# Splitting the first load of a streaming GLU kernel: 16 rows ahead of the launch barrier, 112 rows behind it

## The chip, the cores and the metric

The kernel runs on one core of one Trainium2 chip. The metric is device time in microseconds (us) of one execution.

## The reference

```python
def reference(x):                     # x: float32, 8192 x 8192
    a, b = np.split(x, 2, axis=-1)
    return a * (1 / (1 + np.exp(-b))) # 8192 x 4096
```

The kernel reads 268.4 MB and writes 134.2 MB. Per byte there is little to compute: one sigmoid on ACT (ScalarE), one product on DVE (VectorE).

## The kernel before

The input is cut into 32 tiles of 256 input rows. Each of the 128 partitions of SBUF (the core's on-chip memory) holds two neighbouring input rows, so a **tile row** (one partition's share) is 65,536 bytes, contiguous in memory. Below, "row" means such a tile row. There are two slots for inputs and two for outputs.

```python
    R = 2
    SLOTS = 2
    n_tiles = n_rows // (P * R)
    x_t = x.rearrange("(n p r) m -> n p (r m)", p=P, r=R)
    ...
    xs = [pool.tile([P, R * n_cols], fp32, name=f"x_sb{k}") for k in range(SLOTS)]
    os = [pool.tile([P, R * half], fp32, name=f"o_sb{k}") for k in range(SLOTS)]
    ...
    for i in range(n_tiles):
        ...
        load = nc.sync.dma_start(out=xs[i % SLOTS], in_=x_t[i])
        implied(load, *old["loads"], *old["sigs"])
        now["loads"].append(load)
        ...
        for k, (r, c) in enumerate(parts):          # 4 parts in the first and last tile, else 1
            b = rows[:, r, 1, c]
            sig = nc.scalar.activation(out=b, in_=b, func=SIG)
            mul = nc.vector.tensor_mul(out=packed[:, r, c], in0=rows[:, r, 0, c], in1=b)
            ...
        store(...)                                  # issued from ACT
```

After the build, the first load is moved ahead of the barrier with which all engines start:

```python
def _launch_early(nc):
    SP = mybir.EngineType.SP
    entry, body = (b.instructions for b in nc.main_func.blocks[:2])
    load = next(i for i in body if i.engine == SP and i.opcode == "DMACopy")
    assert not load.sync_info.on_wait
    body.remove(load)
    where = next(k for k, i in enumerate(entry) if i.engine == SP and i.opcode == "Drain")
    entry.insert(where, load)
```

Of the kernel before, what the change touches and what calls it, by code (L numbers as in the profile page):

```python
# [1 line left out]

# [4 lines left out]


def _tiles(ctx, tc, x, out):









    nc = tc.nc
    P = nc.NUM_PARTITIONS  # L20
    DEP = mybir.DependencyInfo(mybir.DependencyClass.Sync, mybir.DependencyReason.DATA)
    fp32 = mybir.dt.float32
    SIG = mybir.ActivationFunctionType.Sigmoid

    n_rows, n_cols = x.shape
    half = n_cols // 2
    R = 2
    SLOTS = 2
    n_tiles = n_rows // (P * R)
    x_t = x.rearrange("(n p r) m -> n p (r m)", p=P, r=R)  # L30
    out_t = out.rearrange("(n p r) m -> n p (r m)", p=P, r=R)

    pool = ctx.enter_context(tc.tile_pool(name="io", bufs=1))
    xs = [pool.tile([P, R * n_cols], fp32, name=f"x_sb{k}") for k in range(SLOTS)]
    os = [pool.tile([P, R * half], fp32, name=f"o_sb{k}") for k in range(SLOTS)]

    def implied(later, *earlier):
        for e in earlier:
            tc.declare_no_dep(later.ins, e.ins, reason="follows from the waits that are kept")

    gone = [{k: [] for k in ("loads", "sigs", "muls", "stores")} for _ in range(SLOTS)]
    last_stores = [[] for _ in range(SLOTS)]
    for i in range(n_tiles):
        old = gone[i % SLOTS]
        freed = last_stores[i % SLOTS]
        now = {k: [] for k in old}
        rows = xs[i % SLOTS].rearrange("p (r h m) -> p r h m", r=R, h=2)
        packed = os[i % SLOTS].rearrange("p (r m) -> p r m", r=R)

        load = nc.sync.dma_start(out=xs[i % SLOTS], in_=x_t[i])  # L50
        implied(load, *old["loads"], *old["sigs"])
        now["loads"].append(load)

        if 0 < i < n_tiles - 1:
            parts = [(slice(0, R), slice(0, half))]
        else:
            w = half // 2
            parts = [
                (slice(r, r + 1), slice(c * w, (c + 1) * w)) for r in range(R) for c in range(2)
            ]  # L60
        def store(cols):
            ins = nc.scalar.dma_start(out=out_t[i, :, cols], in_=os[i % SLOTS][:, cols])  # L62
            now["stores"].append(ins)

        chunks = []
        for k, (r, c) in enumerate(parts):
# [3 lines that stand above are left out]
            implied(sig, *old["sigs"], *old["muls"], *old["loads"])  # L70
            implied(mul, *old["muls"], *old["loads"], *now["loads"])
            by_sigmoid = i % 2 == 1 and len(parts) == 1
            implied(mul, *(s for s in old["stores"] if by_sigmoid or s not in freed))
            if by_sigmoid:
                for s in freed:
                    tc.add_manual_dep(sig.ins, s.ins.name, DEP, reason="frees the output slot")
            tc.keep_in_program_order(sig)
            now["sigs"].append(sig)
            now["muls"].append(mul)
            chunks.append(slice(r.start * half + c.start, r.start * half + c.stop))  # L80
            if i == n_tiles - 1 and k > 0:
                store(chunks[k - 1])
        store(chunks[-1] if i == n_tiles - 1 else slice(0, R * half))
        for s in now["stores"]:
            implied(s, *old["loads"], *old["sigs"], *old["muls"], *now["loads"], *now["sigs"])
        for k in old:
            old[k] += now[k]
        last_stores[i % SLOTS] = now["stores"]
# [15 lines that stand above are left out]
def _close_on_sync(nc):  # L104





    SP, POOL = mybir.EngineType.SP, mybir.EngineType.Pool  # L110
    ACT = mybir.EngineType.Activation
    block = nc.main_func.blocks[2].instructions
    waits = block[0]
    assert waits.engine == SP and waits.opcode == "Drain" and len(waits.sync_info.on_wait) > 1
    pool = [i for i in block if i.engine == POOL]
    drain1, gather1, release1, reset, clear, drain2, gather2, release2 = pool
    assert reset.is_reset_sema and clear.opcode == "ISA"
    others = [i for i in block[1:] if i.engine != POOL]
    arrive = [i for i in others[: len(others) // 2] if i.opcode == "Drain"]
    assert len(arrive) == 4  # L120
    body = nc.main_func.blocks[1].instructions
    last = [i for i in body if i.engine == ACT and i.opcode == "DMACopy"][-1].sync_info.on_update[0].id
    final = [w for w in waits.sync_info.on_wait if w.id == last]
    assert len(final) == 1

    def event(engine, wait, update=()):
        return mybir.InstEventSemaphore(
            name=nc.get_next_instruction_name(),
            engine=engine,
            debug=waits.debug,  # L130
            sync_info=mybir.SyncInfo(on_wait=[wait], on_update=list(update)),
        )

    n = len(block)
    for lo, hi in ((reset.reset_range_start, last), (last + 1, reset.reset_range_stop)):
        if lo < hi:
            nc.gpsimd.sem_clear(range(lo, hi))
    clears = block[n:]
    assert clears and all(i.opcode == "ISA" for i in clears)
    back = mybir.SyncUpdate(  # L140
        sync_type="semaphore",
        id=last,
        ant_name=final[0].ant_name,
        update_mode="sem-sub-imm",
        update_value=final[0].wait_value,
        update_reg=None,
    )
    block[:] = [
        *arrive,
        drain1,  # L150
        gather1,
        *(event(POOL, w) for w in waits.sync_info.on_wait if w.id != last),
        reset,
        *clears,
        drain2,
        event(SP, final[0], [back]),
    ]


@with_exitstack  # L160
def kernel(
    ctx: ExitStack,
    tc: tile.TileContext,
    x: bass.AP,
    out: bass.AP,
):
    nc = tc.nc
    with ExitStack() as pools:
        _tiles(pools, tc, x, out)
    tc.close()  # L170
    tc.compile()
    _launch_early(nc)
    _close_on_sync(nc)


# [1 line left out]
_INS = ['x']  # L177
_OUTS = [((8192, 4096), 'float32')]


# [23 lines left out]
```

## Time and profile before

| | kernel before |
|---|---|
| time, median of the runs beside the changed kernel | 933.84 us |
| span of the profiled execution | 931.7 us |
| DVE / ACT busy | 278.7 / 227.1 us |
| moved by the 16 DMA engines | 402.67 MB, mean 432 GB/s |
| tile 0 landed, first sigmoid | 21.95 us |
| tile 1 landed, second sigmoid | 44.80 us |

The views by stretches count a DMA packet wholly in the stretch where it starts. If a stretch is chosen so that exactly 16 packets start in it (as bytes / 65,536 shows), then share x length is the mean time of one packet.

### The profile page before, as it was taken

What the parts mean: (1) busy time and instruction counts of PE and PEld (TensorE: products, weight loads), DVE (VectorE), ACT (ScalarE), POOL (GpSimd) and SP (SyncE); (2) the same over time, 40 slices, a digit from 0 to 9 for tenths busy, and PEclk for the clock granted to TensorE, in tenths of its full rate; (3) what the DMA queues carried; (4) which work ended last, traced back from release to release, by engine and by line L of the source; (5) the groups of instructions that cost most, each with busy time, mean ns of one, the idle gap of its engine ahead of it and who ended that gap; (6) DMA issues with size and microseconds to landing.
All of it is one profiled execution on the core that took longest, in us unless ns stands there. A gap on an engine that the chain in (4) does not pass through costs nothing.

```text
span 931.7 us, 247 instructions
## 1 busy us (share of the span) xinstructions
DVE 278.7 (30%) x38; ACT 227.1 (24%) x39; POOL 0.2 (0%) x4
## 2 busy tenths in 40 slices
DVE  0333213333133331233312333123331233312333
ACT  1323330233311333113331133311333113332033
POOL 0000000000000000000000000000000000000000
DMA  9999999999999999999999999999999999999999
GB/s 405 428 450 428 422 456 405 450 428 428 450 418 438 428 436 442 428 428 450 447 408 428 442 459 428 413 460 411 450 428 425 453 408 447 428 428 450 425 430 405
DMA packets 9649, 402.67 MB, mean 432 GB/s; under 512 B 1072, under 2 KB 1072, under 8 KB 1072
## 3 DMA queue, kind: packets, MB, share of 16 engines
q1 hardware_dynamic: 4608, 268.44, 66.6%
q10 hardware_dynamic: 5040, 134.22, 33.4%
q14 instruction: 1, 0.01, 0.0%
HBM read 268.44 MB, written 134.22 MB: 432 GB/s over the span
## 4 chain that ended last, share of the span: by engine, by line
DMA 73%; DVE 15%; ACT 12%; issue 0%; ACTq 0%
DMA x_sb<-in_x_dram 73%; DVE o_sb L69 15%; ACT x_sb L68 12%; ACTq L62 0%; ACTq L68 0%
## 5 line engine op out<-in xcount | busy, mean ns | idle before, releaser
L69 DVE TENSOR_TENSOR o_sb<-x_sb 128x8192 f32<-128x8192 f32 (+1 forms) x38 | 278.7, 7344 | 647.1 <-ACT x_sb L68 647.1
L68 ACT ACTIVATE x_sb<-x_sb 128x8192 f32<-128x8192 f32 (+1 forms) x38 | 225.8, 5952 | 695.6 <-DMA x_sb<-in_x_dram 694.4
L68 ACT ACT_TABLE_LOAD x1 | 1.3, 1283 | 0.8 <-PEq L188 0.8
L188 POOL MEMSET const-bfloat16-1.0<- 128x1 bf16 x1 | 0.1, 102 | 0.0
L188 POOL MEMSET const-uint8-127<- 128x1 uint8 x1 | 0.1, 102 | 0.0
L188 POOL MEMSET const-float32-0.0<- 128x1 f32 x1 | 0.1, 99 | 0.2 <-issue 0.2
L188 POOL MEMSET const-float32-1.0<- 128x1 f32 x1 | 0.1, 99 | 0.0
## 6 DMA issues: line engine op xcount, KB each, us to landing
out_dram<-o_sb ACTq DMA_DIRECT2D x31, 4096.0 KB, 34.7
out_dram<-o_sb ACTq DMA_DIRECT2D x4, 1024.0 KB, 5.6
x_sb<-in_x_dram SPq DMA_DIRECT2D x32, 42.2
```

The costliest lines, as they stand in the source:

```text
L68: sig = nc.scalar.activation(out=b, in_=b, func=SIG)
L69: mul = nc.vector.tensor_mul(out=packed[:, r, c], in0=rows[:, r, 0, c], in1=b)
L188: nc = _bacc.Bacc("TRN2", target_bir_lowering=False, num_devices=1)
```

## The change

The intent is to have a small transfer ahead of the barrier, and the bulk behind it. `_launch_early` is untouched and now moves the 16 rows alone.

```diff
+    LEAD = 16
...
-        load = nc.sync.dma_start(out=xs[i % SLOTS], in_=x_t[i])
-        implied(load, *old["loads"], *old["sigs"])
-        now["loads"].append(load)
+        for p in [slice(0, LEAD), slice(LEAD, P)] if i == 0 else [slice(0, P)]:
+            load = nc.sync.dma_start(out=xs[i % SLOTS][p], in_=x_t[i, p])
+            implied(load, *old["loads"], *old["sigs"])
+            now["loads"].append(load)
```

## The prediction

+7.0 us for the lead and +9.7 us for the rest were the author's estimates, and so were the figures that follow from them (9.7 us for a packet of the lead, tile 0 near 38 us or near 29, 941 and 990 us). The -0.3 us for the intended gain was an estimate too, out of the 0.7 us of start-up (3.1 - 2.42). The sum came to -0.3 + 7.0 + 9.7 = +16.4 us, or 950 us, and 949 was stated. "Clash" is the author's word for a part whose packets last longer than the 2.42 us of the full transfer; "lead alone" means that only the 16 rows do.

> **What bounds the kernel now.** I read the page first, then the longer stretches of DMA work, then the first microseconds in order of time, because the change touches nothing after the first tile. The page:
>
> ```profile
> span 931.7 us, 247 instructions
> DVE 278.7 (30%) x38; ACT 227.1 (24%) x39; POOL 0.2 (0%) x4
> DMA  9999999999999999999999999999999999999999
> DMA packets 9649, 402.67 MB, mean 432 GB/s; under 512 B 1072, under 2 KB 1072, under 8 KB 1072
> q1 hardware_dynamic: 4608, 268.44, 66.6%
> ```
>
> No compute engine is busy for a third of the span, while the 16 DMA engines are at nine tenths or more in every slice. The kernel is a stream: 402.67 MB at a nearly constant rate. The view by stretches says how constant; its last two columns are the busy share of the DMA engines and GB/s (a packet counts wholly in the stretch where it starts):
>
> ```profile
> 0.00:0.90 0.90, 0.00 (x0) 0.12 (x1) 0.20 (x4) 1.00 0.00 0
> 0.90:3.00 2.10, 0.00 (x0) 1.16 (x1) 0.00 (x0) 1.00 1.48 499
> 3.00:5.00 2.00, 0.00 (x0) 0.00 (x0) 0.00 (x0) 1.00 1.21 524
> 100.00:900.00 800.00, 241.70 (x28) 196.87 (x28) 0.00 (x0) 1.00 1.00 434
> ```
>
> Between 100 and 900 us the engines are full, at 434 GB/s, or 27.1 for each of the 16. In the stretch from 3 to 5 us 524 GB/s x 2.00 us = 1.05 MB start, which is 16 packets of 65,536 bytes, one per engine, each a whole row of the tile (two rows of the input); they take 1.21 x 2.00 = 2.42 us each, and 65,536 bytes in 2.42 us is again 27.1 GB/s. The first 16 packets take 1.48 x 2.10 = 3.1 us each: a start-up loss of 0.7 us. Nothing moves in the first 0.9 us. Since the engines are never without work afterwards, **the end is the moment when the slowest engine has moved its sixteenth of the bytes**. A microsecond that one engine loses at the start is not won back; a microsecond that ACT or DVE loses is nothing as long as the queue holds work. The order of time near the start shows how much it holds:
>
> ```profile
> 0.78 1.28 ACT L68 ACT_TABLE_LOAD   x1 [0.78 <-PEq L188]
> 21.95 7.31 ACT L68 ACTIVATE x_sb<-x_sb 128x2048 f32<-128x2048 f32 x4 [19.89 <-DMA x_sb<-in_x_dram]
> 23.89 8.90 DVE L69 TENSOR_TENSOR o_sb<-x_sb 128x2048 f32<-128x2048 f32 x4 [23.89 <-ACT x_sb L68]
> 32.82 0.38 ACTq L62 DMA_DIRECT2D out_dram<-o_sb  x1
> 44.80 7.03 ACT L68 ACTIVATE x_sb<-x_sb 128x8192 f32<-128x8192 f32 x1 [15.53 <-DMA x_sb<-in_x_dram]
> ```
>
> Tile 0 has landed at 21.95; its products are done at 32.8, where its store and the load of tile 2 are issued; tile 1 is still arriving, until 44.80. So ACT and DVE have about 12 us of slack in this first round.
>
> [...]every transfer of the kernel before has 128 partitions, so none shows the narrow case. [...]
>
> **The change part by part.** The 8.39 MB load of tile 0 becomes a lead of 16 rows (1.05 MB, before the barrier) and a rest of 112 rows (7.34 MB, behind it). All other instructions keep their order on each engine.
>
> *The barrier.* In the kernel before, the second load is issued at 0.78 us, just behind the barrier; the rest takes that place. The first load, issued at 0.00, moves its first packets at about 1.0 us, so the rest can move at about 1.8 us. The lead keeps every engine busy until 1.0 + 2.4 = 3.4 us at least. So there is no hole: 0 us. One more issue on the sync queue costs about 0.33 us, which lies beside moving data: 0 us.
>
> *The intended gain.* [...]I count -0.3 us.
>
> *The ACT table.* The order of the built program shows that the table load, which waited for nothing, now waits for the transfer of 112 rows[...]. So 1.28 us of table load moves from under the first load to between its landing and the first sigmoid. Against 12 us of slack: 0 us on the end, but it will be visible at the start.
>
> [...]
>
> [...]112 rows over 16 engines is 7 rows each, 16.9 us at 2.42 us a row. [...]
>
> Sum of the likeliest branch: -0.3 + 0 + 0 + 0 + 7.0 + 9.7 = **+16.4 us**, or 950 us. I state **949**, as some of the last term may be evened out.
>
> **The rivals.** (1) *Hidden or neutral.* [...]the time stays at 933 to 935. [...](2) *Lead alone.* [...]about +7 us, 941. (3) *The rest the other way.* [...]near 990. [...]I give this 5%. (4) *The table load becomes the bound*: the 12 us of slack speak against it; it could make 1.3 us at most.
>
> **Range and chances.** I give no clash at all 20%, the lead alone 25%, both clashes 50%, dealt rows 5%. The first three span 933 to 951; [...]the range goes up to 957: **933 to 957**. The line for slower is 933.84 x 1.02 = 952.5, which is 18.7 us, only 2 us above the branch with both clashes: I put 22% above it, 1% on faster (that would take 18.7 us out of a stream at its full rate, of which the change can reach 0.7 us), and 77% within 2%.
>
> **What would show each step.** In the stretches of the changed kernel: if the lead clashes, its 16 packets last about 9.7 us, and hardly a packet starts between 3 and 10 us; if not, the pace of 16 packets per 2.42 us is there from the start. If the rest clashes too, many of its packets last 3 to 5 us, and tile 0 lands near 38 us in place of 21.95; near 29 with the lead alone. The table load must stand right ahead of the first sigmoid, 1.3 us after the landing, and the load of tile 2 must still be issued ahead of tile 1's landing. From 100 us on nothing may differ but a shift: 434 GB/s again. The prediction is wrong if tile 0 lands near 22 us[...] or if a late landing is won back by the end (then the slowest engine is not what sets it).

## More of the kernel before

The page has the span in 40 equal slices; this is its line of GB/s for the kernel before. The reader is to see that the first slice (23 us long) is nearly as full as the others:

```profile
GB/s 405 428 450 428 422 456 405 450 428 428 450 418 438 428 436 442 428 428 450 447 408 428 442 459 428 413 460 411 450 428 425 453 408 447 428 428 450 425 430 405
```

## The result, and the profile after

The changed kernel takes **953.96 us** (median of 5 runs, 953.35 to 954.04) against 933.84 us (5 runs, 933.25 to 934.3). The ratio is 1.0217, with a 95% interval of 1.0205 to 1.0230. Ratios here are the mean time of one kernel's fast runs over that of the other's fast runs of the same rounds, so not quite the ratio of the medians. The change costs 20.1 us, and it is slower by just over 2%.

The page of the changed kernel: the first two slices have lost 47% and 38% of their rate; of the rest only the last is clearly emptier than before (358 against 405).

```profile
span 952.7 us, 250 instructions
GB/s 215 264 440 421 436 444 418 457 417 444 440 418 443 417 458 420 442 418 440 443 417 439 433 447 419 440 435 427 454 414 450 418 436 442 422 455 413 451 440 358
```

The same stretch by stretch. The first eight lines hold 16 packets each: the lead, then the seven steps of the 112 rows. The ninth is the first step of tile 1.

```profile
0.90:3.00 2.10, 0.00 (x0) 0.00 (x0) 0.00 (x0) 1.00 4.08 499
8.50:11.00 2.50, 0.00 (x0) 0.00 (x0) 0.00 (x0) 1.00 2.27 419
15.00:16.10 1.10, 0.00 (x0) 0.00 (x0) 0.00 (x0) 1.00 4.29 953
19.80:20.80 1.00, 0.00 (x0) 0.00 (x0) 0.00 (x0) 1.00 3.16 1049
22.90:25.40 2.50, 0.00 (x0) 0.00 (x0) 0.00 (x0) 1.00 1.54 419
26.70:29.00 2.30, 0.00 (x0) 0.00 (x0) 0.00 (x0) 1.00 1.95 456
30.90:33.60 2.70, 0.00 (x0) 0.00 (x0) 0.00 (x0) 1.00 1.74 388
35.50:38.30 2.80, 0.00 (x0) 0.00 (x0) 0.00 (x0) 1.00 1.62 374
40.00:43.10 3.10, 0.00 (x0) 0.00 (x0) 0.00 (x0) 1.00 0.99 338
100.00:900.00 800.00, 243.37 (x28) 191.51 (x28) 0.00 (x0) 1.00 1.00 434
```

Share x length gives the mean packet of each step. The bill can be written from them:

| step | mean packet after, us | before, us | difference |
|---|---|---|---|
| the lead, 16 rows | 8.57 | 3.11 | +5.5 |
| the 112 rows, steps 1 to 7 | 5.68, 4.72, 3.16, 3.85, 4.49, 4.70, 4.54: sum 31.1 | 7 x 2.42 = 16.9 | +14.2 |
| tile 1, first step | 3.07 | 2.42 | +0.7 |
| sum, before rounding | | | **+20.3** |

That is close to the 20.1 us that were measured. No packet of rows is larger than before and none is added (the only new ones are 16 of 4 bytes); the same packets take longer. From 100 us on the rate is 434 GB/s, as before.

The order of time at the start of the changed kernel shows the landing at 44.07 us instead of 21.95, and the table load (ACT loads the table of the sigmoid) moved right behind it:

```profile
44.07 1.28 ACT L70 ACT_TABLE_LOAD   x1 [44.07 <-DMA x_sb<-in_x_dram]
45.37 7.31 ACT L70 ACTIVATE x_sb<-x_sb 128x2048 f32<-128x2048 f32 x4
56.24 0.37 ACTq L64 DMA_DIRECT2D out_dram<-o_sb  x1
65.72 7.03 ACT L70 ACTIVATE x_sb<-x_sb 128x8192 f32<-128x8192 f32 x1 [13.04 <-DMA x_sb<-in_x_dram]
```

Tile 0 is 22.1 us late, tile 1 is 20.9 us late (65.72 against 44.80). From there the lag stays: in the traces the load of tile 3 is requested 20.9 us later than before and that of tile 31 20.8 us later; the spans differ by 21.0. So nearly all of a loss in the first 43 us is still there at the end, 900 us later. (About 1.2 us of the first tile's delay are given back while tile 1 lands.)

### The profile page after: what moved, and what is told of

Its sections match the earlier page's. It is cut to its first block, busy times and chain, and to the rows that moved or that the text cites. A ratio compares the mean times of both kernels' runs of the same rounds, so it can differ in the third digit from the quotient of the medians.

```text
span 952.7 us, 250 instructions
## 1 busy us (share of the span) xinstructions
DVE 278.6 (29%) x38; ACT 227.0 (24%) x39; POOL 0.2 (0%) x4
## 4 chain that ended last, share of the span: by engine, by line
DMA 71%; DVE 15%; ACT 12%; another core or an unknown queue 1%; issue 0%; ACTq 0%
DMA x_sb<-in_x_dram 71%; DVE o_sb L71 15%; ACT x_sb L70 12%; ACT L70 0%; ACTq L64 0%; ACTq L70 0%
```

## The experiments

Eleven kernels ran, all with correct results. The theory is that which rows a transfer moves together decides how long their packets take. The rivals are the barrier, the number of transfers or their descriptors, the late table load, and the mere fact that a transfer has fewer than 128 rows. The first four runs went together.

### Split by columns instead of rows (e1_cols)

The change with the same two sizes, but every part has all 128 rows. A dependence of the first sigmoid on both parts is added, so that the waits are those of the changed kernel.

```diff
-        for p in [slice(0, LEAD), slice(LEAD, P)] if i == 0 else [slice(0, P)]:
-            load = nc.sync.dma_start(out=xs[i % SLOTS][p], in_=x_t[i, p])
+        full = R * n_cols
+        for p in [slice(0, full // 8), slice(full // 8, full)] if i == 0 else [slice(0, full)]:
+            load = nc.sync.dma_start(out=xs[i % SLOTS][:, p], in_=x_t[i, :, p])
```

> The first load is split by columns instead of rows: 128 rows by 2048 columns ahead of the barrier, 128 rows by 14336 columns behind it. Same bytes in each part (1.05 and 7.34 MB), same two waits, table load as late as in the changed kernel. [...]no packet is stretched and tile 0 lands near 22 us: 933 to 935 us. Rival, the split or the barrier or the late table load costs the time: still 950 or more.

Measured: **933.70 us** against 934.06, ratio 0.9995 (0.9983 to 1.0008): the same. The order of time of this run:

```profile
21.69 1.28 ACT L71 ACT_TABLE_LOAD   x1 [21.69 <-DMA x_sb<-in_x_dram]
33.85 0.38 ACTq L65 DMA_DIRECT2D out_dram<-o_sb  x1
45.08 7.03 ACT L71 ACTIVATE x_sb<-x_sb 128x8192 f32<-128x8192 f32 x1 [14.79 <-DMA x_sb<-in_x_dram]
```

There are two transfers, the barrier between them, and a table load that waits for the landing, and tile 0 lands at 21.69 us. The store of tile 0 goes out at 33.85 us, 1.0 us later than in the kernel before, and the end does not move. So neither the split, nor the barrier, nor the late table load costs time here. Nor does the split gain any: the 0.26 us by which tile 0 lands earlier cannot be seen in the time.

### Two halves of 64 rows (e2_lead64)

```diff
-    LEAD = 16
+    LEAD = 64
```

> Two equal halves of 64 rows. [...]every row takes 2 x 2.42 = 4.84 us and tile 0 takes 8 x 4.84 = 38.7 us instead of 19.3: the last packet ends near 41 us, and the time is 933.8 + 19 = 953. [...]If only the 16 narrow rows matter (the lead alone), +0 to 7 us.

Measured: **953.74 us**, ratio 1.0209 (1.0194 to 1.0225). Two of its eight steps by stretches, each with 16 packets:

```profile
5.90:7.00 1.10, 0.00 (x0) 0.00 (x0) 0.00 (x0) 1.00 4.65 953
11.00:12.10 1.10, 0.00 (x0) 0.00 (x0) 0.00 (x0) 1.00 4.66 953
```

4.65 x 1.10 = 5.1 us for a packet, near the 4.84 us that were expected and about twice the 2.42 us of the full transfer. The trace does not say which engine or row a packet belongs to, so how rows are dealt to engines is not shown.

### 112 rows first, 16 behind (e3_lead112)

```diff
-    LEAD = 16
+    LEAD = 112
```

> 112 rows (0 to 111) ahead of the barrier, 16 rows (112 to 127) behind it: the same two sizes in the other order. [...]slowest engine ends tile 0 near 34 us, +13 us, about 947. [...]7 rows at up to 4.84 us and one at 9.7, near 43 to 45 us, +21 us, about 955. Barrier theory: nearly all of the load is ahead of the barrier, so 934.

Measured: **953.06 us**, ratio 1.0205 (1.0191 to 1.0218). Steps three to six of the 112 rows, and the 16 rows behind them:

```profile
9.70:11.70 2.00, 0.00 (x0) 0.00 (x0) 0.00 (x0) 1.00 2.38 524
14.40:16.40 2.00, 0.00 (x0) 0.00 (x0) 0.00 (x0) 1.00 1.73 524
18.20:20.30 2.10, 0.00 (x0) 0.00 (x0) 0.00 (x0) 1.00 1.74 499
21.70:24.00 2.30, 0.00 (x0) 0.00 (x0) 0.00 (x0) 1.00 1.97 456
...
30.60:33.90 3.30, 0.00 (x0) 0.00 (x0) 0.00 (x0) 1.00 2.43 318
```

The mean packets are 4.76, 3.46, 3.65 and 4.53 us, and 8.0 us for the 16 rows. The faster steps are four and five here, and three and four in the changed kernel (3.16 and 3.85 us). The expectation has two versions: in the first only some packets of a step are slow and tile 0 is done near 34 us, in the second all 16 are held up and it is done near 43 to 45. The wait for it ended at 43.20 us in the trace: the second version is the nearer one.

### Both parts ahead of the barrier (e4_both_early)

```diff
-    load = next(i for i in body if i.engine == SP and i.opcode == "DMACopy")
+    loads = [i for i in body if i.engine == SP and i.opcode == "DMACopy"][:2]
     (each of them is then moved as before)
```

> The changed kernel with both parts issued ahead of the barrier. [...]nothing changes, 954 us (within 1). Rival, the 112 rows lose time because they are issued behind the barrier: back to 934.

Measured: **954.00 us**, ratio 1.0213 (1.0199 to 1.0227). In its order of time both requests of the sync queue are out at 0.83 us (with the second behind the barrier, as in the kernel before, it is 1.10 us):

```profile
0.00 0.83 SPq L52 DMA_DIRECT2D x_sb<-in_x_dram  x2
```

The barrier has no part in the loss.

### The narrow lead alone, and its control (e5_extra16, e6_extra_cols)

These start from the kernel before. One more transfer fills part of tile 1's slot ahead of the barrier; tile 1 overwrites it later, after a wait. The two differ in its shape alone.

```diff
+    nc.sync.dma_start(out=xs[1][0:16], in_=x_t[1, 0:16])                                  # e5_extra16
+    nc.sync.dma_start(out=xs[1][:, 0 : R * n_cols // 8], in_=x_t[1, :, 0 : R * n_cols // 8])  # e6_extra_cols
     for i in range(n_tiles):
```

> The kernel before with one transfer more: rows 0 to 15 of tile 1 (1.05 MB) are loaded ahead of the barrier and overwritten later by the whole tile 1; the first load is whole again. Measures the narrow lead by itself. [...]the time is the kernel before plus about 8.5 to 10 us: 942 to 944. If a narrow transfer cost no more than its bytes: plus 2.4 us.

> Control for the extra 16 rows: the same 1.05 MB more, but as 128 rows by 2048 columns of tile 1. [...]plus 2.4 us: about 936.3.

Measured: **941.55 us** for the 16 rows and **935.82 us** for the same bytes over 128 rows, beside 933.37 for the kernel before; ratios 1.0086 (1.0071 to 1.0101) and 1.0026 (1.0011 to 1.0041). In the trace of the first:

```profile
0.90:2.00 1.10, 0.00 (x0) 1.10 (x1) 0.00 (x0) 1.00 7.73 953
```

Its 16 packets take 8.5 us on average. The bytes by themselves cost 2.45 us, the shape 5.7 us more, which agrees with the +5.5 of the lead in the bill above. The first expectation (942 to 944) was slightly too high.

### 64 rows at full speed, and 64 rows with two slow packets in a step (p1_mid64, p2_one_pair)

As the last pair, with other rows: 32 to 95, and 28 to 91. The second expectation has two versions, both of 953 us: two packets of a step are slow, or all are.

```diff
+    nc.sync.dma_start(out=xs[1][32:96], in_=x_t[1, 32:96])    # p1_mid64
+    nc.sync.dma_start(out=xs[1][28:92], in_=x_t[1, 28:92])    # p2_one_pair
```

> The kernel before with rows 32 to 95 of tile 1 (4.19 MB) loaded once more ahead of the barrier. [...]packets of 2.42 us, plus 4 x 2.42 = 9.7 us, about 943.5. Rival, a transfer of fewer than 128 rows is slow[...]: packets near 5.1 us as with rows 0 to 63, plus about 20 us.

> The same with rows 28 to 91[...]. [...]plus 4 x 4.84 = 19 us (953), because the slowest engine sets the end; the packets tell them apart. [...]14 packets of each step last 2.42 us and 2 last 4.84. All engines coupled: all packets last about 4.8 us.

Measured: **943.63 us** with rows 32 to 95, 10.3 us above the kernel before, ratio 1.0108 (1.0093 to 1.0123). Two of the four steps:

```profile
4.20:5.10 0.90, 0.00 (x0) 0.00 (x0) 0.00 (x0) 1.00 2.71 1165
6.60:7.60 1.00, 0.00 (x0) 0.00 (x0) 0.00 (x0) 1.00 2.42 1049
```

2.71 x 0.90 = 2.44 and 2.42 us a packet: half of the rows, and the 2.42 us of the full transfer. Rows 0 to 63 took 5.1 us a packet. Here the number of rows is not what matters; which rows they are is.

With rows 28 to 91 the expected time was clearly missed: **981.57 us**, ratio 1.0512 (1.0491 to 1.0534), 48 us instead of 19. Until tile 0 begins, the packets are as in the first version of the expectation: in the second step 14 of them last 2.42 us, two 5.1. But the other 14 engines then go on to tile 0, and the pair with the slow packets ends its fourth row some 14 us after them. Meanwhile three packets at a time last 7.0 to 8.3 us, and those of the other 13 engines last 3.01 us for most of that time. Tile 2 is requested 25 us later than before, tile 31 45 us later: unlike in the changed kernel the lag grows. The three stretches are the pair in its second step (2 packets, 2.13 x 0.30 x 16 / 2 = 5.1 us), one step of the 13 (3.50 x 0.70 x 16 / 13 = 3.0 us), and 100 to 300 us, where this run moves less than the 434 GB/s of the kernel before:

```profile
5.60:5.90 0.30, 0.00 (x0) 0.00 (x0) 0.00 (x0) 1.00 2.13 437
20.70:21.40 0.70, 0.00 (x0) 0.00 (x0) 0.00 (x0) 1.00 3.50 1217
100.00:300.00 200.00, 60.85 (x7) 49.20 (x7) 0.00 (x0) 1.00 1.00 419
```

### The same with a wait (p5_one_pair_wait)

To see whether the unevenness makes the lag grow, tile 0 is requested only when the 64 rows have landed.

```diff
+    probe = nc.sync.dma_start(out=xs[1][28:92], in_=x_t[1, 28:92])
...
+        if i == 0:
+            tc.add_manual_dep(load.ins, probe.ins.name, DEP, reason="after the probe")
```

> The run with rows 28 to 91 ended 48 us late, of which 25 us were there when tile 2 was requested and the rest grew tile by tile. Here tile 0 is requested only when those rows have landed, so all engines start it level[...]. If the growth came from the unevenness (two or three engines 12 us behind the others): 4 rows of the pair at about 5.1 us and some 4 us until the next transfer moves, plus 23 to 27 us, 957 to 960, and no growth after tile 0. If the transfer itself leaves something slow behind: again about 980. In the probe, 14 engines should have packets of 2.42 us and two of 4.8 to 5.1.

Measured: **955.80 us** against 933.27, ratio 1.0232 (1.0215 to 1.0249), a little below the 957 to 960 that were expected. The lag is 22.7 us when tile 2 is requested and 24.0 us at tile 31, so most of the growth is gone with the unevenness. Why uneven engines lose more as the tiles go by was not found out. Two stretches of the second step of the probe, the first with 14 packets in it, the second with 2 (1019 GB/s x 0.90 us and 437 x 0.30 us over 65,536 bytes):

```profile
4.30:5.20 0.90, 0.00 (x0) 0.00 (x0) 0.00 (x0) 1.00 2.35 1019
6.10:6.40 0.30, 0.00 (x0) 0.00 (x0) 0.00 (x0) 1.00 2.14 437
```

2.35 x 0.90 x 16 / 14 = 2.42 us and 2.14 x 0.30 x 16 / 2 = 5.1 us. **In this run two packets of a step are slow, 5.1 us, and the other 14 are not, 2.42 us.**

### Another 64 rows, and single steps (p3_two_pairs, p4_steps)

Both are read from their packets, not from their times. The first is as `p1_mid64` with rows 40 to 103. The second sends five transfers of 16 rows, each waiting for the one before, ahead of tile 0, which waits for the last (not shown in the cut):

```diff
+    probe = None
+    for start, step in ((11, 7), (16, 7), (18, 7), (32, 4), (0, 1)):
+        part = slice(start, start + 15 * step + 1, step)
+        ins = nc.sync.dma_start(out=xs[1][part], in_=x_t[1, part])
+        if probe is not None:
+            tc.add_manual_dep(ins.ins, probe.ins.name, DEP, reason="one probe at a time")
+        probe = ins
```

Each expectation has two versions, in this order: a few packets of a step are slow, or all 16 are.

> As the runs with rows 32 to 95 and 28 to 91, but rows 40 to 103: [...]12 packets of 2.42 us and 4 of about 4.84 in each step. [...]all near 4.7. The end is late in either case, 953 or, like the run with one pair, later.

> The kernel before with five probes ahead of the first load, one at a time, 16 rows (one per engine) each, overwritten later: rows 11+7e[...], 16+7e[...], 18+7e[...], 32+4e[...], 0 to 15[...]. Read from the packets of each probe, not from the time. [...]2.4 to 3.1 us in the first and fourth; in the second four packets near 4.8 and twelve near 2.4 to 3; in the third two near 4.8; in the fifth about 9.7. [...]all packets of the second near 4.7, all of the third near 3.0 to 3.8.[...]

Rows 40 to 103 (952.95 us), the third and fourth step:

```profile
10.70:11.70 1.00, 0.00 (x0) 0.00 (x0) 0.00 (x0) 1.00 5.22 1049
15.90:16.90 1.00, 0.00 (x0) 0.00 (x0) 0.00 (x0) 1.00 5.22 1049
```

All 16 packets of each step take 5.2 us (5.21 to 5.23 in the trace), where the first version of the expectation had four slow ones and twelve of 2.42 us. The five single steps (969.91 us), in order:

```profile
1.30:2.00 0.70, 0.00 (x0) 0.70 (x1) 0.00 (x0) 1.00 4.40 1498
6.80:7.60 0.80, 0.00 (x0) 0.00 (x0) 0.00 (x0) 1.00 5.58 1311
14.00:15.00 1.00, 0.00 (x0) 0.00 (x0) 0.00 (x0) 1.00 3.24 1049
21.00:22.00 1.00, 0.00 (x0) 0.00 (x0) 0.00 (x0) 1.00 2.92 1049
25.80:26.90 1.10, 0.00 (x0) 0.00 (x0) 0.00 (x0) 1.00 7.72 953
```

| the 16 rows, e = 0 to 15 | mean packet, us |
|---|---|
| 11 + 7e | 3.1 |
| 16 + 7e | 4.5 (3.7 to 5.1) |
| 18 + 7e | 3.2 |
| 32 + 4e | 2.9 |
| e | 8.5 |

The first 16 packets of the kernel before, also from a standstill, take 3.1 us, so those of the first and the fourth set are no slower. With rows 16 + 7e all 16 are slow (3.7 us and more). The author took rows 16 + 7e and 18 + 7e for the first and the third step of the 112 rows. The trace does not name the rows of a packet, so that is not shown; but the steps are 5.68 and 3.16 us in the changed kernel, and the sets, taken out of it, 4.5 and 3.2 us: one slow and one faster in both.

## Why the prediction was right or wrong

- **What sets the end.** Right: DMA is the bound (share 1.00 from 100 to 900 us), ACT and DVE have slack (24% and 30% busy), and the loss at the start was not won back. The lag was 20.9 us at tile 1 and 20.8 us at tile 31. `p2_one_pair` shows a limit of this step: there, with uneven engines, the lag grew from 25 us at tile 2 to 45 us at tile 31.
- **The barrier, 0 us.** Right, by `e4_both_early` (954.00 us) and `e1_cols` (933.70 us).
- **The ACT table, 0 us.** Right: in `e1_cols` it stands behind the landing and the time is that of the kernel before. In the changed kernel the load of tile 2 was still requested at 56.2 us, ahead of tile 1's landing at 65.7.
- **The intended gain, -0.3 us.** Not found. The lead's first packets start in the same stretch from 0.9 to 3 us, and with a lead of 128 rows (`e1_cols`, 933.70 us) nothing measurable is gained.
- **The lead, +7.0 us.** Slightly too large: +5.5 us in the packets, 5.7 us in the pair of controls. The prediction set the time of a whole transfer against the 3.1 us of a mean packet; in the trace the 16 packets are through 9.7 us after the first one starts, but last 8.57 us on average.
- **The rest, +9.7 us.** This is the term that was mis-sized. It was the author's estimate, in which a few engines at a time run at half speed; that part rested on what was not shown. What failed was to let the others run on at 2.42 us: the 16 packets of a step take 4.5 us on average with rows 16 + 7e (`p4_steps`) and 5.2 us with rows 40 to 103 (`p3_two_pairs`). The mean of the seven steps' packets adds up to 31.1 us instead of 16.9, so the term is +14.2 us. Tile 0 landed at 44 us instead of "near 38". The two figures are not of one kind, either: +9.7 us was the slowest engine of a replay, while +14.2 us is the mean of all 16, which end their seventh row within 3.0 us of each other. So not a few engines were late, but all.
- **Time and chances.** 953.96 us lies within 933 to 957, 5 us above the stated 949. It does so in part by luck: the replay's slowest engine happened to stand in for a loss that all engines have, and the top of the range is an allowance that was not worked out. The outcome slower by over 2% had been given 22%; the missing 5 us were just what lifts it over that line.
- **The rivals.** Neutral and the lead alone are refuted by where tile 0 landed (44 us, not 22 or 29), the rest the other way, near 990 us, by the time (953.96 us). `e2_lead64`, with other rows, is not neutral either (5.1 us a packet, not 2.42). The table load as the bound is refuted by `e1_cols`.

What stays open is why some sets of rows are slow, and why with one set two packets of a step are slow and the others are not (rows 28 to 91: 5.1 and 2.42 us), while with another all 16 are (rows 40 to 103: 5.2 us). No run here shows the mechanism. Open also is why the lag of `p2_one_pair` grows.

One question stands untested. In every run row p of a tile goes to partition p, so the runs show which rows are slow together, but not whether that comes from where they are written or from where they are read. Loading one set of rows into other partitions would tell.

No version tried beats the kernel before; the split by columns equals it.

## What to carry to other kernels

If a transfer has to be split in a stream that is bound by DMA, try the split along the free dimension first, with all 128 partitions in each part: here the same bytes cost 0 us that way (933.70 us against 934.06) and 20 us by rows (953.96 against 933.84). If a row split cannot be avoided, measure the packets of the rows in question, since here 64 rows went at full speed (32 to 95, 2.42 us a packet) or at half (0 to 63, 5.1 us), and 64 rows that left the engines uneven (28 to 91) cost 48 us. When adding up such losses, do not assume that only a few packets of a step are slowed: with rows 28 to 91 it was two of 16, with rows 40 to 103 all. Measure a single step first.
